# One transformer layer with 32 experts on one core: LayerNorm rows in pieces between the products, the last columns in 256, 128 and 128, part of LayerNorm 2 as a product with a diagonal

## The chip, the cores and the metric

The kernel runs on one core of a Trainium2 chip, as one launch. The metric is the device time of an execution in microseconds (us); lower is better. The profile shows TensorE (PE, with its weight loads as PEld), VectorE (DVE), ScalarE (ACT), GpSimd (POOL) and SyncE (SP), which here issues nearly all transfers from HBM.

## What is computed

One layer over 256 latent tokens of width 1024, in float32, cut to what matters here:

```
o    = bidirectional retention(q, k, v)            # 8 heads, over chunks of 128 tokens
ret  = silu(g) * head_norm(o)                      # norm over the 256 values of a head
z    = silu(layernorm(depthwise_conv(glu)))        # 31 taps
mix  = (ga * (ret @ w_ret_out) + gb * (z @ w_conv_out + b)) @ w_mix_out + b_mix
h    = layernorm(ALPHA * h + gt_m * mix) * ln1_g + ln1_b
u    = modulate(h)
y    = sum over 32 experts of combine[:, e] * ((silu(u @ w_gate[e]) * (u @ w_up[e])) @ w_down[e])
out  = layernorm(ALPHA * h + gt_f * y) * ln2_g + ln2_b
```

A token goes to one group of 8 experts and to two experts in it. All 32 experts' weights (6 MB each, 192 MB in all) are read from HBM.

## The kernel before, in words

Three stages follow one another. The **front** (0 to about 500 us) computes everything up to the router, with float32 products done as three products of high and low parts (`mm3`, lines 94 to 96). The **experts** follow (500 to about 943 us) as 16 pairs `e0 = 0, 2, ... 30`, and then a **tail** (LayerNorm 2 and the store).

*Loads.* `plan` lists the experts' weights as 192 slabs of 1 MB: for each pair eight slabs of `gate` and `up`, then four of `down` (column half `cb` 0 of both experts, then `cb` 1). `slots` names the SBUF buffer of each slab in advance, and `load_to` (line 1016) issues them in that order on SP's queue, which waits for a buffer to be read out before it issues into it. From slab 147 on the buffers form a cycle of 16, earlier one of 18; `NCYC` sets where the shorter cycle begins, since buffers are then wanted for `lnv` (LayerNorm rows) and `yacc` (the sum that becomes the output).

*Front.* `run_steps` goes through a list of steps: each slice of weights is split into high and low parts (`emit`, lines 162 and 163: an ACT copy and a DVE subtraction, `qg`, `qro`, `qco`), `LEAD` slices ahead of PE. `weave` and `call` put the steps of retention, conv norm and gates between one another at positions `APOS`, `TPOS`, ... For the last pair of heads (`p = 3`) `post` (line 667) computes the reciprocal root of the variance by a bit trick and three Newton steps on DVE (lines 113 to 119), while the same for the conv norm (`crs`, 128 x 256) is done by twelve POOL operations (`newton`, lines 820 to 824); `post2` normalises `sr`, which `ret_t` transposes (`rt`, `rT`) as the operand of the product `ya`. `conv_norm` multiplies `zp` by `crs`, `conv_act` makes `zs`, `zh`, `zl`, operands of the product `yb` with the slices `qco` of `wco`. `rows_load` (line 922) broadcasts three rows over the partitions: `b_mix_out`, and two rows of `arow`, a small HBM scratch that POOL writes once the adaLN columns `secs` are there.

*A pair of experts* (`expert_pair`): `hidden` multiplies the gathered 64 tokens of each expert by `gate` and `up` (`gu`, line 1375); `turn` transposes (`ht`); `place` makes the one-hot matrix `sT` that puts the 64 + 64 rows back to their tokens, and the weights `ws` (`st`, lines 1450 and 1452); two down products `dn` (line 1485) are scaled to high and low parts `dh`, `dl` (lines 1497, 1498), which `scatter` of the next pair adds up (`y`, line 1416). Every second pair also gathers the tokens of the next four experts (`ga`, line 1355). PSUM has two banks `mi` for everything small (`ht`, `st`, `dn`, rows), two `gu`, four `y`.

*LayerNorm rows.* The gain and bias rows lie in one partition of `lnv`; a product with a row of ones (`oner`) spreads a row over the 128 partitions. At the end of pair 24 (`LNS[2]`) four such products `l1r` of 512 columns and eight DVE operations make `yacc` out of `xn` and LayerNorm 1's rows. After pair 28 comes the `If` on `cnt_i` (line 1628; not taken here), then four products `l2r` (line 1657) spread LayerNorm 2's rows, and pair 30 begins.

*The last pair* has no scatter into other pairs: after `flush` it runs its down products in pieces of 512, 256 and 256 columns (`p0`, then `dn_1_0`, `dn_1_1`), each weighed (`ds`), put back (`y`), added into `yacc` and sent through `bn_stats` in quarters. Lines 1664 to 1679 finish: `rstd_pair` with a square root on ACT and one Newton step, then half the rows on DVE, half on ACT, POOL and DVE, each quarter stored from SP.

`keep_clock` adds products that nobody reads in the router's waits (`KC0` to `KC4`).

## Time and profile before

| | |
|---|---|
| median of 3 runs | 975.26 us (974.23 to 975.6) |
| the profiled execution | 975.05 us, of which 973.0 us from the first to the last instruction |
| mean granted TensorE clock | 0.984 |
| PE busy | 928.3 us, 95% |
| DVE, ACT, POOL busy | 518.5, 313.2, 100.6 us |
| moved from and to HBM | 294.92 MB, 303 GB/s on the mean, about 420 GB/s while the experts run |

So 2 us lie outside the span. PE is busy nearly all the time and the transfers are at their rate for nearly half of it, so the shares alone do not say which of the two sets the end: that is read stage by stage.

### The profile page before, as it was taken

How to read it: one execution, taken by the hardware profiler on the slowest of the kernel's cores; microseconds unless marked ns; L12 is line 12 of the kernel's file. 1: busy time of each engine (PE TensorE's matmuls, PEld its weight loads, DVE VectorE, ACT ScalarE, POOL GpSimd, SP SyncE). 2: the span in 40 equal slices, each digit the busy share in tenths (PEclk: the TensorE clock that was granted, in tenths of full speed). 3: DMA queues.
4: the chain of work that ended last, by engine and by line, in shares of the span. 5: the costliest groups of instructions: out<-in, count | busy, mean ns of one | idle time of the engine just before them, and what ended most of it. 6: DMA issues, size and time to landing. Idle time of an engine off the chain costs nothing. (4 is left out here: it accounts for less than half of the span.)

```text
span 973.0 us, 15303 instructions
## 1 busy us (share of the span) xinstructions
PE 928.3 (95%) x6327; PEld 688.2 (71%) x6327; DVE 518.5 (53%) x1000; ACT 313.2 (32%) x459; POOL 100.6 (10%) x114
## 2 busy tenths in 40 slices
...
GB/s 352 419 234 252 83 93 194 256 141 184 114 205 224 44 303 228 206 155 313 369 366 314 423 421 421 420 420 421 420 420 422 420 420 420 420 421 420 419 302 44
DMA packets 48744, 294.92 MB, mean 303 GB/s; under 512 B 10304, under 2 KB 10352, under 8 KB 14368
## 3 DMA queue, kind: packets, MB, share of 16 engines
...
q14 instruction: 21, 0.17, 0.0%
HBM read 292.77 MB, written 1.12 MB: 302 GB/s over the span
## 5 line engine op out<-in xcount | busy, mean ns | idle before, releaser
L1375 PE MATMUL gu<-wgate,xe 128*64 128x256 f32 x1024 | 123.0, 391 | 0.7 <-DMA wgate<-in_w_exp_gate_dram 0.5
L1375 PE MATMUL gu<-wup,xe 128*64 128x256 f32 x1024 | 117.7, 380 | 3.4 <-DMA wup<-in_w_exp_up_dram 3.4
L1485 PE MATMUL dn<-wdown,hT 128*64 128x512 f32 (+1 forms) x528 | 117.1, 583 | 3.6 <-DVE hT L1443 2.5
L335 DVE SCALAR_TENSOR_TENSOR slab<-zp,taps,slab 128x256 f32<-128x256 f32 x232 | 109.2, 525 | 0.0
L1375 PEld LDWEIGHTS gu<-wgate,xe 128*64 128x64 f32 x1024 | 74.6, 140 | 45.3 <-issue 9.9
L1381 DVE TENSOR_TENSOR h<-h,gu 128x256 f32<-128x256 f32 x32 | 13.5, 421 | 171.9 <-ACT h L1380 171.9
L1375 PEld LDWEIGHTS gu<-wup,xe 128*64 128x64 f32 x1024 | 73.9, 137 | 41.6 <-DMA wup<-in_w_exp_up_dram 6.6
L1485 PEld LDWEIGHTS dn<-wdown,hT 128*64 128x64 f32 x528 | 40.3, 137 | 68.2 <-issue 58.6
L1380 ACT ACTIVATE h<-gu 128x256 f32<-128x256 f32 x32 | 12.3, 384 | 205.5 <-PE gu L1375 205.5
L1498 DVE SCALAR_TENSOR_TENSOR dl<-dn,ws,ohq 128x512 fp32r<-128x512 f32 x30 | 22.5, 751 | 94.0 <-ACT ohq L1497 94.0
L1497 ACT ACTIVATE ohq<-dn,ws 128x512 fp32r<-128x512 f32 x30 | 20.6, 687 | 130.1 <-PE dn L1485 127.4
L1355 PEld LDWEIGHTS ga<-ohq,xh 128*128 128x128 f32 x224 | 27.9, 188 | 15.9 <-issue 11.1
L95 PE MATMUL ya<-rT,qro 128*128 128x256 f32 x128 | 36.7, 287 | 2.5 <-DVE rT L726 2.5
L75 POOL DMA_DIRECT2D lnv<-in_ln_g_dram x2 | 1.0, 521 | 367.3 <-PE dn L1485 302.8
L96 PE MATMUL glu<-ulh,qz 128*128 128x256 f32 x128 | 36.4, 284 | 1.9 <-DVE qz L163 1.9
L96 PE MATMUL gt<-ulh,qg 128*128 128x256 f32 x128 | 36.2, 283 | 1.9 <-DVE qg L163 1.9
L94 PE MATMUL glu<-ulh,qz 128*128 128x256 f32 x128 | 37.2, 291 | 0.2 <-ACT qz L162 0.2
L96 PE MATMUL ya<-rT,qro 128*128 128x256 f32 x128 | 36.6, 286 | 0.8 <-DVE qro L163 0.8
L1362 DVE TENSOR_SCALAR xe<-ga,cf 128x256 f32<-128x256 f32 x32 | 17.4, 544 | 37.2 <-ACT xe L1365 36.3
L94 PE MATMUL ya<-rT,qro 128*128 128x256 f32 x128 | 37.0, 289 | 0.0
L1355 PE MATMUL ga<-ohq,xh 128*128 128x256 f32 x224 | 33.6, 293 | 3.4 <-DVE dl L1498 3.4
L94 PE MATMUL gt<-ulh,qg 128*128 128x256 f32 x128 | 36.7, 287 | 0.0
...
## 6 DMA issues: line engine op xcount, KB each, us to landing
wgate<-in_w_exp_gate_dram SPq DMA_DIRECT2D x64, 1024.0 KB, 19.8
wup<-in_w_exp_up_dram SPq DMA_DIRECT2D x64, 1024.0 KB, 19.8
wdown<-in_w_down_dram SPq DMA_DIRECT2D x62, 1024.0 KB, 19.8
wa<-in_w_ada_r_dram SPq DMA_DIRECT2D x16, 1024.0 KB, 4.9
wa<-in_w_ada_m_dram SPq DMA_DIRECT2D x8, 1024.0 KB, 14.5
wro<-in_w_ret_out_dram SPq DMA_DIRECT2D x8, 1024.0 KB, 6.9
wg<-in_w_gates_dram SPq DMA_DIRECT2D x8, 1024.0 KB, 7.2
wz<-in_w_glu_dram SPq DMA_DIRECT2D x5, 1024.0 KB, 13.1
```

Source lines behind the costliest of these rows:

```text
L94: T.matmul(ps, st[0], mv[0], start=start, stop=False)
L95: T.matmul(ps, st[0], mv[1], start=False, stop=False)
L96: T.matmul(ps, st[1], mv[0], start=False, stop=stop)
L335: V.scalar_tensor_tensor(dst, zp[:, ct, j:j + NT], taps[:, ct, j:j + 1], ac[ct], op0=ALU.mult, op1=ALU.add)
L1355: T.matmul(ps[:, kk], halves[k // 4][:, s, t, P * (k % 4):P * (k % 4) + P], ohr[:, t], start=(t == 0 and s == 0), stop=(t == 1 and s == 1))
L1362: V.tensor_scalar(xe[c][:, k], ps[:, kk], fsc[:, k:k + 1], fsh[:, k:k + 1], op0=ALU.mult, op1=ALU.add)
L1375: T.matmul(ps[64 * hf:64 * hf + 64, j], xe[c][:, k, CAP * i:CAP * i + CAP], w[:, k % 4, NT * hf:NT * hf + NT], start=start, stop=stop)
L1380: S.activation(h, ps[:, 0], AF.Silu)
L1381: V.tensor_mul(h, h, ps[:, 1])
L1485: T.matmul(ps[64 * x:64 * x + 64], hT[x][:, ch % 2, 64 * (ch // 2):64 * (ch // 2) + 64], w, start=(ch == 0), stop=(ch == 3))
L1497: S.activation(dh, ps, AF.Copy, scale=ws)
L1498: V.scalar_tensor_tensor(dl, ps, ws, dh.bitcast(F32), op0=ALU.mult, op1=ALU.subtract)
```

## The change

The places it touches, and the diff cut to its core.

- *Conv and head norm of `p = 3`*: the reciprocal roots come from ACT's square root, a DVE reciprocal and one Newton step (`rstd_pair`, `conv_root`, `conv_rstd`); the twelve POOL operations are gone; `post2` follows at once, with two of its four operations on ACT; the transposes `rt` come one position earlier.
- *`rows_load`*: the two `arow` broadcasts go to POOL's queue.
- *Mix and router*: the last half of `mx` is kept in two banks of 256 columns, each added as it is done; the constants of `keep_clock` fall; the group's one-hot `og` and a copy of the identity (`iw`) go to POOL.
- *`place`*: identity and router weights lie side by side in `iw`, two products of 192 columns in place of two of 128 and two of 4.
- *LayerNorm rows*: `lnv` and `yacc` are taken at pair 18 in place of pairs 20 and 24, and the 16-slab cycle begins at slab 129. The rows come in 8 + 8 pieces of 256 columns (ACT copy and DVE subtraction of one partition, two products, two DVE operations for LayerNorm 1 or one ACT copy for LayerNorm 2), one at each call of `row()`: four per pair, in pairs 20 and 22, then 24 and 26. The blocks `l1r` and `l2r` are gone.
- *The last pair*: the last 512 columns in pieces of 256, 128, 128 (`ENDS`), with a weight layout of their own, and six of the eight `bn_stats` ahead of the last piece.
- *LayerNorm 2*: two products put the bias into the banks `fo` ahead of time; a diagonal matrix of the reciprocal roots then multiplies the centred rows of the second token half on PE, and ACT copies the sum out. POOL has no part in it.

```diff
-NPOS, APOS, TPOS, QPOS, AHEAD = 7, 9, 7, 5, ()
+NPOS, APOS, TPOS = 7, 9, 6
-NCYC = 130
+NCYC = 112
-LNS = 20, 26, 24, 28
-KC0, KC1, KC2, KC3, KC4 = 0, 2, 3, 4, 4
+LNS = 18, 20, 22, 24
+KC0, KC1, KC2, KC3, KC4 = 0, 0, 2, 2, 3
+ENDS = (0, 256), (256, 128), (384, 128)
...
@@ retain(p): post
-                more = conv_rstd()
...
+            if p < 3:
+                rstd(rs, mv[:, :, 1], 4, f"hn{p}", fill)
+            else:
+                rstd_pair(rs, mv[:, :, 1], "hn3", 4, conv_root)
+            V.scalar_tensor_tensor(nb, mv[:, :, 0], -1.0, rs, op0=ALU.mult, op1=ALU.mult)
+            box["n"] = mv, rs, nb
+            if p == 3:
+                post2()
+                conv_rstd()
...
-            for i in range(4):
+            for i in (1, 0, 3, 2):
                 hh, t = divmod(i, 2)
                 o = sr[:, 1, t, hh * NT:(hh + 1) * NT]
-                V.tensor_scalar(o, box[hh][:, t], mv[:, i, 0:1], rs[:, i:i + 1], op0=ALU.subtract, op1=ALU.mult)
+                if t:
+                    S.activation(o, box[hh][:, t], AF.Identity, scale=rs[:, i:i + 1], bias=nb[:, i:i + 1])
+                else:
+                    V.tensor_scalar(o, box[hh][:, t], mv[:, i, 0:1], rs[:, i:i + 1], op0=ALU.subtract, op1=ALU.mult)
...
+    def conv_root():
+        nbox["rs"], nbox["h"], ve = row1("crs"), row1("crsh"), row1("crsv")
+        V.tensor_scalar(ve, nbox["var"], 1.0 / D, EPS, op0=ALU.mult, op1=ALU.add)
+        S.activation(nbox["rs"], ve, AF.Sqrt)
+        V.tensor_scalar(nbox["h"], ve, -0.5, None, op0=ALU.mult)
+
     def conv_rstd():
...
-            for _ in range(3):
-                G.tensor_mul(t, crs, crs)
-                G.tensor_mul(t, t, ve)
-                G.tensor_scalar(t, t, -0.5, 1.5, op0=ALU.mult, op1=ALU.add)
-                G.tensor_mul(crs, crs, t)
...
+        V.reciprocal(crs, crs)
+        V.tensor_mul(t, crs, crs)
+        V.tensor_mul(t, t, nbox["h"])
+        V.scalar_tensor_tensor(crs, t, 1.5, crs, op0=ALU.add, op1=ALU.mult)
...
     def rows_load(_):
         bcast(tmp[:, 0], a["b_mix_out"][0], D)
-        bcast(tmp[:, 1], arow[0], D)
-        bcast(gtf, arow[1], D)
+        bcast(tmp[:, 1], arow[0], D, nc.gpsimd)
+        bcast(gtf, arow[1], D, nc.gpsimd)
...
@@ expert_pair: place
             for t in range(2):
-                T.matmul(pt[:, t * P:(t + 1) * P], oh[t], identr, start=True, stop=True)
-            for t in range(2):
-                T.matmul(pt[:, NT:NT + 4], oh[t], Wr[:, t, e0 // 2], start=(t == 0), stop=(t == 1))
+                T.matmul(pw[:, t], oh[t], iw[:, t], start=True, stop=True)
...
             hs.append(hidden(e0))
+            row()
             next(side, None)
             hs.append(hidden(e0 + 1))
+            row()
...
                 V.scalar_tensor_tensor(dl, ps, ws, dh.bitcast(F32), op0=ALU.mult, op1=ALU.subtract)
                 places[e0][1][cb] = dh, dl
+                row()
...
@@ expert_pair, last pair
-        down_half(0)
+        down_piece(*ENDS[0])
         for t in range(2):
             py = bank("y", f"y{e0}_0_{t}")
             T.matmul(py, sT[:, t * P:(t + 1) * P].bitcast(F32), ds_[0], start=True, stop=True)
             V.tensor_add(yacc[:, t, 0:512], yacc[:, t, 0:512], py)
-        product(ps[1], 1, half[1])
-        for q in range(2):
+        down_piece(*ENDS[1])
+        add_piece(*ENDS[0])
+        for q in range(3):
             for t in range(2):
                 stats(t, q)
-        down_scale(1)
...
+        down_piece(*ENDS[2])
+        add_piece(*ENDS[1])
+        add_piece(*ENDS[2])
+        for t in (1, 0):
+            stats(t, 3)
...
+    def pieces(n):
+        box = {}
+        def split(i, c):
+            row = lnv[0:1, i, 256 * c:256 * c + 256]
+            h = box["h"] = sb.tile([P, 2, 256], F32R, tag="rope", name=f"lnh{n}{i}{c}", bufs=1)
+            S.activation(h[0:1, 0], row, AF.Copy)
+            V.tensor_sub(h[0:1, 1], row, h[0:1, 0].bitcast(F32))
+        def use(i, c):
+            cs = slice(256 * c, 256 * c + 256)
+            ps = bank("mi", f"ln{n}{i}{c}")[:, 0:256]
+            for j in range(2):
+                T.matmul(ps, oner[0:1], box["h"][0:1, j], start=(j == 0), stop=(j == 1))
+            if n:
+                S.activation(lnv[:, i, cs], ps, AF.Copy)
+                return
...
+    def row():
+        if rows:
+            rows.pop(0)()
...
-        if e0 == LNS[2]:
...
-                    T.matmul(ps, onef[0:1], lnv[0:1, i, cs], start=True, stop=True)
...
-                            V.scalar_tensor_tensor(yk[:, t], pk, ALPHA, xn[:, t, cb], op0=ALU.mult, op1=ALU.mult)
...
+        for n in range(2):
+            if e0 == LNS[2 * n]:
+                rows.extend(pieces(n))
+                rows.pop(0)()
...
@@ LayerNorm 2
-    V.scalar_tensor_tensor(nb2, mv2[:, :, 0], -1.0, rs2, op0=ALU.mult, op1=ALU.mult)
...
-    for E, t, cb in ((V, 0, 0), (V, 0, 1), (G, 1, 1), (V, 1, 0)):
...
+    for cb in range(2):
+        T.matmul(fo[cb], ident, lnv[:, 1, halves[cb]], start=True, stop=False)
...
+    rstd_pair(rs2, mv2[:, :, 1], "l2", 2, lambda: center(1, 0))
+    diag = row1("diag", (P, P))
+    V.tensor_scalar(diag, ident, rs2[:, 1:2], None, op0=ALU.mult)
+    center(1, 1)
+    for cb in range(2):
+        o = yacc[:, 1, halves[cb]]
+        T.matmul(fo[cb], diag, o, start=False, stop=True)
+        S.activation(o, fo[cb], AF.Copy)
+    for cb in range(2):
+        center(0, cb)
+        o = yacc[:, 0, halves[cb]]
+        V.scalar_tensor_tensor(o, o, rs2[:, 0:1], lnv[:, 1, halves[cb]], op0=ALU.mult, op1=ALU.add)
+    for t, cb in ((1, 0), (0, 0), (1, 1), (0, 1)):
+        send(t, cb)
```

The product order on PE (the rows of pair 20 on the changed side are typical of pairs 20 to 26). Before, at the end of pair 24 and the start of pair 26:

```order
L1485 MATMUL dn_1_7123<-wdown_1_6992,hT_7099 64x512
L1645 MATMUL l1r_7150<-lnv,oner 128x512
L1645 MATMUL l1r_7154<-lnv,oner 128x512
L1645 MATMUL l1r_7158<-lnv,oner 128x512
L1645 MATMUL l1r_7162<-lnv,oner 128x512
L1375 MATMUL gu_7182<-wgate_0_6994,xe_6817 64x256 x8
L1375 MATMUL gu_7182<-wgate_1_6996,xe_6817 64x256 x8
L1375 MATMUL gu_7182<-wup_0_6998,xe_6817 64x256 x8
L1375 MATMUL gu_7182<-wup_1_7000,xe_6817 64x256 x8
```

Now, from pair 20's first products on (`ln` are the two products of a piece of a row, `lnh` its high and low parts):

```order
L1383 MATMUL gu_6658<-wup_0_6439,xe_6458 64x256 x8
L1383 MATMUL gu_6658<-wup_1_6441,xe_6458 64x256 x8
L1644 MATMUL ln_6694<-lnh_6645,oner 128x256 x2
L1383 MATMUL gu_6702<-wgate_0_6443,xe_6458 64x256 x8
L1383 MATMUL gu_6702<-wgate_1_6445,xe_6458 64x256 x8
L1383 MATMUL gu_6702<-wup_0_6447,xe_6458 64x256 x8
L1383 MATMUL gu_6702<-wup_1_6449,xe_6458 64x256 x8
L1644 MATMUL ln_6738<-lnh_6699,oner 128x256 x2
L1424 MATMUL y_0_5177<-ohq,sT_6573 128x512
L1424 MATMUL y_0_5177<-dl_0_6590,sT_6573 128x512
```

The four `l1r` that stood in one block are gone, and a piece `ln` stands behind each `gu` group and, further down, behind each `dn` of these pairs.

SP's order around the rows of `arow`. Before:

```order
L78 DMA tmp<-in_b_mix_out_dram 128x1024
L78 DMA tmp<-arow 128x1024
L78 DMA gtf<-arow 128x1024
L72 DMA wco_4326<-in_w_conv_out_dram 128x2048
L72 DMA wco_4387<-in_w_conv_out_dram 128x2048
L72 DMA wgate_0_4452<-in_w_exp_gate_dram 128x2048
```

Now, on SP:

```order
L79 DMA tmp<-in_b_mix_out_dram 128x1024
L73 DMA wco_4324<-in_w_conv_out_dram 128x2048
L73 DMA wco_4385<-in_w_conv_out_dram 128x2048
L73 DMA wgate_0_4450<-in_w_exp_gate_dram 128x2048
L73 DMA wm_0_4452<-in_w_mix_out_dram 128x2048
```

and on POOL:

```order
L900 TENSOR_TENSOR sg_3499<-sg_3499,yaT 128x1024
L76 DMA arow<-secs 128x2x4 x2
L79 DMA tmp<-arow 128x1024
L79 DMA gtf<-arow 128x1024
L900 TENSOR_TENSOR sg_4165<-sg_4165,yaT 128x1024
L930 TENSOR_TENSOR tmp<-tmp 128x1024
```

The two broadcasts moved from SP, where they stood ahead of the conv output weights `wco`, to POOL, behind its own write of `arow`.

DVE's order around the norm of retention's last heads (`qg`, `qro` are the low parts of weight slices that PE waits for). Before:

```order
L117 SCALAR_TENSOR_TENSOR hn3t<-rs_3645 128x4
L118 TENSOR_TENSOR hn3t<-hn3t,hn3v 128x4
L119 SCALAR_TENSOR_TENSOR rs_3645<-hn3t,rs_3645 128x4
L163 TENSOR_TENSOR qg_2_3686<-wg_1_3684,qg_2_3686 128x1024
L697 TENSOR_SCALAR sr_3336<-o_3623,mv_3644,rs_3645 128x256 x2
L697 TENSOR_SCALAR sr_3336<-o_3632,mv_3644,rs_3645 128x256 x2
L700 TENSOR_TENSOR sr_3336<-sr_3336 128x2x256 x2
L163 TENSOR_TENSOR qg_3_3722<-wg_1_3684,qg_3_3722 128x1024
L163 TENSOR_TENSOR qro_0_3753<-wro_0_3751,qro_0_3753 128x1024
```

Now:

```order
L146 SCALAR_TENSOR_TENSOR rs_3650<-hn_2_3662,rs_3650 128x4
L687 SCALAR_TENSOR_TENSOR nb_3651<-mv_3649,rs_3650 128x4
L701 TENSOR_SCALAR sr_3338<-o_3625,mv_3649,rs_3650 128x256
L701 TENSOR_SCALAR sr_3338<-o_3634,mv_3649,rs_3650 128x256
L704 TENSOR_TENSOR sr_3338<-sr_3338 128x2x256 x2
L825 RECIPROCAL crs<-crs 128x256
L826 TENSOR_TENSOR crst<-crs 128x256
L827 TENSOR_TENSOR crst<-crst,crsh 128x256
L828 SCALAR_TENSOR_TENSOR crs<-crst,crs 128x256
L166 TENSOR_TENSOR qg_2_3690<-wg_1_3688,qg_2_3690 128x1024
L166 TENSOR_TENSOR qg_3_3720<-wg_1_3688,qg_3_3720 128x1024
L728 TENSOR_TENSOR rT_3749<-rt_0_3750,rT_3749 128x512
```

The slice `qg_2` moved from ahead of the normalisation `sr` to behind it and behind the four operations on `crs`; `qg_3` follows it at once.

## Rows read from the trace of the kernel before

**Rows 1.** The busy time of each engine in stretches of the span (start:end in us, length; busy us and instructions of PE, PEld, DVE, ACT, POOL; the granted TensorE clock; the mean busy share of the DMA engines; GB/s).

```profile
400.00:405.00 5.00, 2.46 (x12) 2.08 (x11) 4.30 (x3) 4.40 (x7) 1.48 (x1) 0.76 0.87 303
405.00:410.00 5.00, 5.00 (x40) 5.00 (x40) 2.87 (x5) 3.15 (x6) 0.00 (x0) 0.90 0.35 147
430.00:435.00 5.00, 5.00 (x45) 5.00 (x44) 1.95 (x2) 4.13 (x5) 0.00 (x0) 1.00 0.00 0
450.00:455.00 5.00, 1.79 (x8) 1.59 (x9) 2.45 (x2) 3.65 (x5) 1.80 (x4) 0.88 1.01 425
455.00:460.00 5.00, 5.00 (x36) 5.00 (x35) 2.90 (x4) 1.49 (x3) 1.65 (x4) 0.78 1.02 406
525.00:530.00 5.00, 5.00 (x26) 2.89 (x24) 0.75 (x1) 0.69 (x1) 0.00 (x0) 1.00 0.31 128
944.00:945.00 1.00, 1.00 (x14) 0.64 (x12) 0.29 (x1) 0.00 (x0) 0.00 (x0) 1.00 0.08 33
945.00:950.00 5.00, 4.06 (x29) 2.28 (x27) 0.85 (x3) 1.87 (x3) 0.00 (x0) 1.00 0.00 0
```

**Rows 2.** The page's list of DMA issues: instructions of this kind, KB each, median us from issue to landing.

```profile
wgate<-in_w_exp_gate_dram SPq DMA_DIRECT2D x64, 1024.0 KB, 19.8
```

**Rows 3.** PE's timeline, the first product of three consecutive pairs (e0 = 16, 18, 20): start, us, instruction, records merged into the row.

```profile
718.72 3.69 PE L1375 MATMUL gu<-wgate,xe 128*64 128x256 f32 x32
...
742.71 3.62 PE L1375 MATMUL gu<-wgate,xe 128*64 128x256 f32 x32
...
771.82 3.68 PE L1375 MATMUL gu<-wgate,xe 128*64 128x256 f32 x32
```

**Rows 4.** PE's timeline from the second half of the gate product of expert 25 to the start of pair 26 (in brackets the idle time before a row and what ended it).

```profile
840.23 1.95 PE L1375 MATMUL gu<-wgate,xe 128*64 128x256 f32 x16 [0.54 <-DMA wgate<-in_w_exp_gate_dram]
...
845.20 1.95 PE L1375 MATMUL gu<-wup,xe 128*64 128x256 f32 x16 [0.54 <-DMA wup<-in_w_exp_up_dram]
...
858.73 1.12 PE L1645 MATMUL l1r<-lnv,oner 1*128 1x512 f32 x2
...
865.42 6.04 PE L1375 MATMUL gu<-wgate,xe 128*64 128x256 f32 x32
```

**Rows 5.** PE's timeline from the end of pair 28 to the last product.

```profile
922.90 5.40 PE L1657 MATMUL l2r<-lnv,oner 1*128 1x512 f32 x8 [1.81 <-DVEq L1628]
928.24 5.36 PE L1375 MATMUL gu<-wgate,xe 128*64 128x256 f32 x32
...
948.45 5.96 PE L1485 MATMUL dn<-wdown,hT 128*64 128x512 f32 x32
954.34 1.98 PE L1526 MATMUL y<-ds,sT 128*128 128x512 f32 x4
956.25 1.95 PE L1485 MATMUL dn<-wdown,hT 128*64 128x256 f32 x16
```

**Rows 6.** The page's list of costliest groups, the low part `dl` of a down product (busy us, mean ns of one | idle before, and what ended it).

```profile
L1498 DVE SCALAR_TENSOR_TENSOR dl<-dn,ws,ohq 128x512 fp32r<-128x512 f32 x30 | 22.5, 751 | 94.0 <-ACT ohq L1497 94.0
```

**Rows 7.** DVE's timeline in the tail.

```profile
952.72 0.75 DVE L1489 SCALAR_TENSOR_TENSOR ds<-dn,ws,gtf 128x512 f32<-128x512 f32 x1 [3.73 <-PE dn L1485]
...
956.96 1.40 DVE L1509 BATCH_NORM_STATS2 st<-yacc 128x6 f32<-128x256 f32 x4
...
961.61 0.38 DVE L1664 BATCH_NORM_AGGREGATE mv<-st 128x2 f32<-128x24 f32 x2
...
962.47 0.17 DVE L140 RECIPROCAL rs<-rs 128x2 f32<-128x2 f32 x1
...
963.33 0.75 DVE L1677 SCALAR_TENSOR_TENSOR yacc<-yacc,mv,lnv 128x512 f32<-128x512 f32 x1
...
968.84 0.69 DVE L1675 TENSOR_TENSOR yacc<-yacc,lnv 128x512 f32<-128x512 f32 x1
```

**Rows 8.** SP's timeline around the rows of `arow` (instructions that issue transfers).

```profile
421.65 0.60 SPq L78 DMA_DIRECT2D tmp<-in_b_mix_out_dram  x1
441.19 0.33 SPq L78 DMA_DIRECT2D tmp<-arow  x1
...
442.37 0.86 SPq L72 DMA_DIRECT2D wco<-in_w_conv_out_dram  x2
```

**Rows 9.** PE's waits from 380 to 460 us (total us, times, longest).

```profile
PE yb L94 <- ACT qco L162: 2.6, 1, 2.6
PE ya L95 <- DVE rT L726: 2.5, 1, 2.5
PE gt L96 <- DVE qg L163: 1.9, 2, 1.6
```

**Rows 10.** DVE's timeline around the norm of retention's last pair of heads.

```profile
386.60 0.60 DVE L118 TENSOR_TENSOR hn3t<-hn3t,hn3v 128x4 f32<-128x4 f32 x1
...
391.03 1.89 DVE L697 TENSOR_SCALAR sr<-o,mv,rs 128x256 f32<-128x256 f32 x4
...
399.35 3.21 DVE L163 TENSOR_TENSOR qro<-wro,qro 128x1024 fp32r<-128x1024 f32 x1
```

**Rows 11.** POOL's timeline there.

```profile
398.75 2.73 POOL L829 TENSOR_TENSOR zp<-zp,crs 128x1024 f32<-128x1024 f32 x1
```

**Rows 12.** ACT's timeline there.

```profile
401.21 1.28 ACT L838 ACT_TABLE_LOAD   x1
402.50 0.60 ACT L838 ACTIVATE zs<-zp,pcol 128x256 f32<-128x256 f32 x1
```

More of the change, by code (lines that the diff above doesn't have):

```diff
@@ L707, in retain_all @@
         step(lambda _: post2())
-    last = []
     def ret_t(p, c2):
@@ L1478, in expert_pair, with product @@
         ds_ = {}
-        def product(ps, cb, cs):
+        def product(ps, cb, c):
             for ch in range(4):
                 for x in range(2):
-                    w = wts[e0 + x, "down", cb][:, ch]
-                    w = w[:, cs.start // 256] if cs.stop - cs.start == 256 else w
+                    w = wts[e0 + x, "down", cb]
+                    w = w[c][:, ch] if last and cb else w[:, ch]
                     T.matmul(ps[64 * x:64 * x + 64], hT[x][:, ch % 2, 64 * (ch // 2):64 * (ch // 2) + 64],
@@ L1499, in expert_pair @@
                 places[e0][1][cb] = dh, dl
+                row()
             next(side, None)
             return
-        half = [slice(256 * q, 256 * q + 256) for q in range(2)]
-        ps = [bank("gu", f"dn{e0}_1_{q}")[:, 0:256] for q in range(2)]
         ds_[1] = sb.tile([P, 512], F32, tag="b2", name=f"ds{e0}_1", bufs=2)
@@ L1617, in tile_block, with one_, go @@
     lnv = yacc = None
+    def pieces(n):
[13 more added lines that the diff above has]
+                return
+            r, o = divmod(c, 2)
+            for t in range(2):
+                if i == 0:
+                    V.scalar_tensor_tensor(yacc[:, t, cs].rearrange("p (q k) -> p k q", k=4),
+                                           ps.rearrange("p (q k) -> p k q", k=4), ALPHA,
+                                           xn[:, t, r, :, 64 * o:64 * o + 64], op0=ALU.mult, op1=ALU.mult)
+                else:
+                    V.scalar_tensor_tensor(yacc[:, t, cs], ps, ALPHA, yacc[:, t, cs], op0=ALU.mult, op1=ALU.add)
+        todo = [(i, c) for i in range(2) for c in range(4)]
+        def one_(j):
+            def go():
+                if j:
+                    use(*todo[j - 1])
+                if j < len(todo):
+                    split(*todo[j])
+            return go
+        return [one_(j) for j in range(len(todo) + 1)]
+    def row():
+        if rows:
+            rows.pop(0)()
+    rows = []
     for e0 in range(0, NE, 2):
```

196 lines of the change are left out of this document (85 added, 111 removed).

## The prediction

> **What bounds the kernel now.** I read the stretches of the span first, then PE's waits and timeline from the end backwards, then the front.
>
> In the experts' stage two clocks run against each other. One is the transfers: a slab of 1 MB becomes usable every 2.49 us (840.23 and 845.20 are two slabs apart, each product behind an idle of 0.54 us for its slab [rows 4]), so a pair of 12 slabs takes 29.9 us. Counted on from there, slab n is usable at 840.23 + 2.49 (n - 149): the first of pair 20 (n = 120) at 768.0, of pair 30 (180) at 917.4, the last up slab (187) at 934.9, the last `cb0` slab (189) at 939.8, the very last (191) at 944.8. The bytes confirm it: 8% of the rate from 944 to 945, nothing after [rows 1]. The other clock is PE: a pair without gathers takes 742.71 - 718.72 = 24.0 us, one with them 771.82 - 742.71 = 29.1 [rows 3]. PE starts pair 20 3.8 us behind the transfers, and by 840 it waits for each slab.
>
> It loses that step at the end of pair 24. The four `l1r` and their DVE operations run from 858.73 to 865.42, and the next gate product takes 6.04 us where it took 3.62 [rows 3, 4]. Slab 156 was usable at 857.7, so pair 26 starts 7.7 us late. Before pair 30 PE idles 1.81 us, spends 5.40 on `l2r` and 5.36 on a gate product [rows 5]: that product begins at 928.24, 10.8 after its slab. The last down product begins at 948.45, with its second expert's operand some 0.5 later, so I count from 949.0; its slabs were there at 939.8. Hence **at the end PE, not the transfers, is late, by 9.2 us**.
>
> The transfers' own schedule was fixed much earlier. From 430 to 435 nothing is moved, from 525 to 530 31% [rows 1]: buffers come free as PE reads them. From about 535 the rate is full to the end, so whatever PE gains before then moves every later slab with it.
>
> **The change, part by part.**
>
> *LayerNorm rows.* Removed: the two blocks. Added: 16 pieces over pairs 20 to 26. A piece's two products cover half of an `l1r`'s columns (a row of two records is 1.12 us for 512 [rows 4], at a low clock): 0.3 to 0.6 us. Larger is what they wait for. With two `mi` banks a piece between `dn_0` and `dn_1` makes `dn_1` take the bank of `dn_0`, so PE waits until `dl` has read it: 0.75 us [rows 6] behind the piece's own products, about 1 us a pair. In pair 20 `yacc`'s first write waits for the buffer's last reader, about 1.5; in pair 22 the gathers queue behind a bank that DVE must clear, about 2. I take +2.8, +4, +2, +2.2 us for the four pairs, 11 in all. Transfers set 917.4 - 771.8 = 145.6 us from PE's start of pair 20 to slab 180; PE needs 3 x 24.0 + 2 x 29.1 = 130.2 there. The slack of 15.4 holds 11, and pair 28, which has no piece, ends in waiting. So pair 30 follows the transfers: slab 187 at 934.9, 16 records of 1.9 us, 2.0 for `h` and its transposes, 938.8; slab 189 at 939.8. **The last down product starts at 939.8, not 949.0: -9.2** (bounds: -7, if 2 us of wait stay in pair 30; -9.2, since slab 189 excludes more).
>
> *Fewer buffers.* Sixteen slabs ahead are 39.8 us of transfers; one takes 19.8 from issue to landing [rows 2]. The schedule starves only if PE falls some 19 us behind; the worst I find is 4. Cost 0, hidden under that margin.
>
> *Place.* Two products of 192 columns for two of 128 and two of 4: about -0.25 us a pair, nothing where PE waits for slabs.
>
> *`arow` on POOL's queue.* SP issues `b_mix_out` at 421.65 and then stands until 441.19, since `arow` is not there; the two `wco` slices go out at 442.37 [rows 8]. They arrive late: PE idles 2.6 us for `qco` [rows 9], and the clock of the next ten microseconds is 0.88 and 0.78 [rows 1], which is 0.6 + 1.1 = 1.7 us of full speed. With SP free, `wco` lands in the idle stretch around 430. POOL has only the `sg` product queued behind, which waits for ACT later. Gain 4.3; bounds 0 (another wait, on DVE's low parts, takes the place) and 4.5.
>
> *Norm of the last heads.* DVE's operations are stretched beside POOL's Newton steps: a 128 x 4 multiply takes 0.60, then `qro` 3.21 beside POOL's 2.73 [rows 10, 11]. PE waits 1.9 for `qg` and 2.5 for `rT` [rows 9] and then runs at 0.76 and 0.90 [rows 1], 1.7 more: 6.1 at most. Now POOL's twelve are gone, but `qg_2` stands behind the normalisation and four `crs` operations. Adding up DVE's queue from the variance (385.7): small operations 1.9, ACT's root 0.4, `sr` 0.8 (half of 1.89 [rows 10]) and 1.4, `crs` 1.6, `qg_2` 1.2 gives 393.0, where it ended at 391.1: a new stall of about 2 us takes the place of the old 1.9. What goes is the `rT` stall. ACT has one more table load, 1.28 us [rows 12], ahead of `zs`, which pushes the conv operands by about 1. I take -2.5, bounds -0.5 and -5.
>
> The Trainium skill speaks against a part of this: "VectorE: DVE Perf Modes" (First, the fixed hardware budget) says that Reciprocal iterates with a repeat count of 8. By it the one over 256 columns would be an estimated 256 x 8 / 0.96 GHz = 2.1 us; no row here is wide enough to show it (0.17 us for two columns [rows 7], as short as any operation). In my sum it stands at 0.3, the time of a plain operation of that width; by the page `qg_2` ends 1.8 later and the term falls to about -0.7. The same holds for ACT: "ScalarE: Activation LUTs" (What ACT_TABLE_LOAD costs) adds a drain of 1.38 us to each switch, but `zs` begins at 402.50, 0.01 after the load's end [rows 12], so the row decides.
>
> *Mix and router.* Earlier sums for the norm, fewer fillers, `og` on POOL: -0.2 (bounds -0.7 and +0.3, a clock that sinks with the fillers gone); `st` in pair 0 -0.3.
>
> Together **the front moves every slab by 2.5 + 4.3 + 0.5 = 7.3 us** (3 to 10).
>
> *Tail.* From the start of the last down product to the end of the last DVE operation it is 968.84 + 0.69 - 949.0 = 20.5 us. In the new order the pieces of 128 columns need 16 records each; at 256 columns they take 1.95 / 16 = 0.12 [rows 5]. I take 0.11, since the weight load does not shrink (bounds 0.06, by columns, and 0.12). Counted from the start: 512 and 256 columns to 5.3, `y` to 7.2 (its 1.98 [rows 5]), the first piece of 128 to 9.0, its `y` to 10.0, two adds to 10.9, six statistics of 0.35 [rows 7], which now stand ahead of the last `ds`, to 13.0, that `ds` 0.4, four small adds 1.1, two statistics 0.7: `bn_aggr` starts at 15.2, in place of 961.61 - 949.0 = 12.6. The end is shorter: centre 0.75 under ACT's root, five small operations 1.0, the diagonal 0.3, then five operations of 0.75 [rows 7], with `aggr`'s 0.4 and the first two steps' 0.2 some 6.4 in place of 7.9. Sum 15.2 + 6.4 = 21.6, **+1.1**, which I round to +1.2 for the stores, whose order changes (bounds 0 and +2.5, when the diagonal's products on PE, at low clock, come last).
>
> **Sum.** 975.05 - 9.2 - 7.3 + 1.2 = **959.8 us**. The profiled execution lies 0.2 under the median of the runs, 975.26.
>
> **Rivals.**
> 1. *The front gives nothing*: `qg_2` behind a slow reciprocal stalls PE as long as `rT` did, and `yb` waits for ACT's later `zs` whatever `wco` does. For it: DVE and ACT are full there. Against: a stall of 2.6 has a transfer alone behind it. 975.05 - 9.2 + 1.2 = 967.1. Chance 0.15.
> 2. *The pieces keep PE behind*: at 1.4 us each they cost 22, 6.6 over the slack, and pair 30 starts late as now. For it: two `mi` banks. Against: only four a pair, with ACT and DVE idle. 975.05 - 9.2 + 6.6 - 7.3 + 1.2 = 966.4. Chance 0.1.
> 3. *The tail gets shorter*: pieces of 128 by columns, full clock: -1.5 in place of +1.2, 957. Chance 0.1.
> 4. *Slower: each piece costs over 1.9 us*, in pairs 20 to 26, since ACT's and DVE's split, PE and the copy out of the bank run one after another with PE standing behind them. The point is where 16 pieces eat the slack, the old lateness and the front's gain less the tail: (15.4 + 9.2 + 7.3 - 1.2) / 16 = 1.9. At 2.2, 35.2 - 15.4 = 19.8 late: 975.05 + 10.6 - 7.3 + 1.2 = 979.6, and close to the 19 us at which buffers run out too. For it: an `l1r` with its DVE work cost 6.7 / 4 = 1.7 [rows 4]. Against: the split is done a position ahead, and only two of four calls in a pair stand before a product that needs the same bank. Chance 0.04.
> 5. *Nothing moves the end*: front and rows each give back what they take, 975. Chance 0.03.
>
> The forecast itself has 0.58, with a range of its own of 955 to 964. Faster by over 0.2% (2 us, about what a measurement of this kernel tells from no change) is the forecast and rivals 1 to 3: 0.92; within it 0.04; slower 0.04. For 8 in 10 the range runs from 954 to 969, the bounds of the front and rivals 1 and 2 inside.
>
> **What would show it.** In the changed trace: no PE wait for `qco` near 450, `wco` issued before 430, transfers flowing from 427 on; full rate about 7 us earlier than 535; pair 30's gate products each behind a wait for their slab; the last byte near 937 and the last down product within 3 us of slab 189; 21 to 22 us from its start to the last DVE operation. I am wrong if PE has no slab wait in pair 28, if the idle before `ya` or `yb` is over 3 us, or if the last byte lands later than 942.

## The result and the profile after

The changed kernel takes 962.57 us (median of four runs, 961.19 to 963.65) where the kernel before takes 975.10 beside it: a ratio of 0.9872, with a 95% interval of 0.9855 to 0.9889. In a second measurement, further down, the ratio was 0.9863 (0.9840 to 0.9886). The forecast was 959.8, with a range of 954 to 969. The profiled execution takes 962.40 us with a span of 960.6, 12.4 less than before.

Three places carry the argument. First the front, in the same view as [rows 1]: busy us and instructions of PE, PEld, DVE, ACT and POOL, the granted clock, DMA share, GB/s.

```profile
395.00:400.00 5.00, 4.36 (x24) 4.36 (x25) 5.00 (x4) 0.11 (x1) 2.62 (x1) 0.66 0.15 23
400.00:405.00 5.00, 5.00 (x45) 5.00 (x44) 3.64 (x5) 3.67 (x6) 0.00 (x0) 1.00 0.87 329
...
430.00:435.00 5.00, 5.00 (x44) 5.00 (x44) 1.84 (x4) 4.13 (x5) 0.00 (x0) 1.00 0.32 134
490.00:495.00 5.00, 4.14 (x19) 3.05 (x18) 3.52 (x15) 4.47 (x4) 1.00 (x4) 0.61 1.00 405
495.00:500.00 5.00, 5.00 (x18) 3.83 (x19) 0.54 (x1) 0.97 (x2) 0.00 (x0) 0.71 1.01 424
```

The low clock of 400 to 410 and of 450 to 460 is gone. Two new stretches of it have come: 395 to 400, and the router from 490 to 500, where it was 1.00 before. PE's waits from 380 to 460 (to be laid beside [rows 9]) show one stall in place of three, and a wait for `zl` of 1.1 us where it was 0.2:

```profile
PE gt L97 <- DVE qg L166: 3.2, 1, 3.2
PE yb L96 <- DVE zl L842: 1.1, 1, 1.1
```

SP's timeline around `wco`: no row of `arow`, and the first `wco` slice goes out 15 us earlier than in [rows 8].

```profile
422.18 0.38 SPq L79 DMA_DIRECT2D tmp<-in_b_mix_out_dram  x1
427.27 7.60 SPq L73 DMA_DIRECT2D wco<-in_w_conv_out_dram  x2
434.96 0.39 SPq L73 DMA_DIRECT2D wgate<-in_w_exp_gate_dram  x1
```

Then PE at the end, in the view of [rows 5]:

```profile
917.02 3.67 PE L1383 MATMUL gu<-wgate,xe 128*64 128x256 f32 x32 [1.80 <-DVEq L1684]
...
935.41 1.07 PE L1495 MATMUL dn<-wdown,hT 128*64 128x512 f32 x2
936.78 5.34 PE L1495 MATMUL dn<-wdown,hT 128*64 128x512 f32 x30 [0.30 <-DMA wdown<-in_w_down_dram]
...
946.05 1.09 PE L1495 MATMUL dn<-wdown,hT 128*64 128x128 f32 x16
```

The last down product now waits for its slab (189, which lands at 936.6), with PE idle for 0.3 us: at that place the transfers are the later of the two. And DVE's tail, in the view of [rows 7]:

```profile
940.44 0.75 DVE L1499 SCALAR_TENSOR_TENSOR ds<-dn,ws,gtf 128x512 f32<-128x512 f32 x1 [4.49 <-PE dn L1495]
...
951.00 0.38 DVE L1719 BATCH_NORM_AGGREGATE mv<-st 128x2 f32<-128x24 f32 x2
...
956.10 0.75 DVE L1731 SCALAR_TENSOR_TENSOR yacc<-yacc,rs,lnv 128x512 f32<-128x512 f32 x1
```

**Where the time went.** I followed the start of the same products in both traces (us, before and after):

| PE reaches | before | after | shift |
|---|---|---|---|
| `o` of the last pair of heads | 377.49 | 378.62 | +1.13 |
| the gate products behind the first `yb` | 426.94 | 427.47 | +0.53 |
| `mx` | 466.46 | 461.55 | -4.91 |
| the router's first gather `ga` | 499.73 | 494.65 | -5.08 |
| the first gate product of pair 0 | 503.35 | 499.90 | -3.45 |
| the first `ds` (DVE) of the last pair | 952.72 | 940.44 | -12.28 |
| end of the span | 973.0 | 960.6 | -12.40 |

So the front gave 3.45 us, the rows 12.28 - 3.45 = 8.83, and the tail 0.12. The forecast had 7.3, 9.2 and -1.2. The two executions begin alike (PE's short stall near 50 stands at 49.15 and 49.24), so these shifts hold to 0.1 us.

Two parts of the change show neither a gain nor a loss. From the first gate product of pair 0 to that of pair 20 it is 268.47 us in both kernels, so the shorter `place` did not speed up these ten pairs. And slab 189 lands at 936.6 in place of 940.1, earlier by as much as the front gave: the transfers lost nothing by the fewer buffers.

### The profile page after: what moved, and what is told of

It reads as the page before. It is cut to its first block, busy times and chain, and to the rows that moved or that the text cites. A ratio compares the mean times of both kernels' runs of the same rounds, so it can differ in the third digit from the quotient of the medians.

```text
span 960.6 us, 15381 instructions
## 1 busy us (share of the span) xinstructions
PE 919.7 (96%) x6339; PEld 684.2 (71%) x6339; DVE 525.4 (55%) x1022; ACT 324.5 (34%) x492; POOL 92.5 (10%) x104
## 3 DMA queue, kind: packets, MB, share of 16 engines
q0 software_dynamic: 1072, 1.74, 0.7%
## 4 chain that ended last, share of the span: by engine, by line
PE 77%; DMA 13%; DVE 6%; ACT 3%; issue 1%; POOL 0%; DVEq 0%; ACTq 0%; SPq 0%; POOLq 0%
PE gu L1383 18%; PE dn L1495 9%; DMA wdown<-in_w_down_dram 4%; DMA wgate<-in_w_exp_gate_dram 4%; DMA wup<-in_w_exp_up_dram 4%; PE o L663 3%; PE y L1424 2%; PE ga L1363 2%; PE glu L97 2%; PE glu L95 2%; PE adp L773 2%; PE glu L96 1%; PE gt L97 1%; PE sc L644 1%; PE gt L95 1%; PE gt L96 1%
## 5 line engine op out<-in xcount | busy, mean ns | idle before, releaser
L1495 PE MATMUL dn<-wdown,hT 128*64 128x512 f32 (+2 forms) x544 | 116.9, 571 | 8.6 <-DVE hT L1451 4.4
L1383 PE MATMUL gu<-wgate,xe 128*64 128x256 f32 x1024 | 117.7, 381 | 1.8 <-DVEq L1684 1.8
L336 DVE SCALAR_TENSOR_TENSOR slab<-zp,taps,slab 128x256 f32<-128x256 f32 x232 | 114.7, 547 | 0.0
L1383 PEld LDWEIGHTS gu<-wgate,xe 128*64 128x64 f32 x1024 | 72.4, 137 | 40.7 <-issue 2.8
L97 PE MATMUL ya<-rT,qro 128*128 128x256 f32 x128 | 36.1, 282 | 0.8 <-DVE qro L166 0.8
L96 PE MATMUL gt<-ull,qg 128*128 128x256 f32 x128 | 36.6, 286 | 0.0
L95 PE MATMUL ya<-rT,qro 128*128 128x256 f32 x128 | 36.2, 283 | 0.0
L96 PE MATMUL glu<-ull,qz 128*128 128x256 f32 x128 | 36.1, 282 | 0.0
```

The costliest lines, as they stand in the source:

```text
L95: T.matmul(ps, st[0], mv[0], start=start, stop=False)
L96: T.matmul(ps, st[0], mv[1], start=False, stop=False)
L97: T.matmul(ps, st[1], mv[0], start=False, stop=stop)
L336: V.scalar_tensor_tensor(dst, zp[:, ct, j:j + NT], taps[:, ct, j:j + 1], ac[ct], op0=ALU.mult, op1=ALU.add)
L1383: T.matmul(ps[64 * hf:64 * hf + 64, j], xe[c][:, k, CAP * i:CAP * i + CAP], w[:, k % 4, NT * hf:NT * hf + NT], start=start, stop=stop)
L1495: T.matmul(ps[64 * x:64 * x + 64], hT[x][:, ch % 2, 64 * (ch // 2):64 * (ch // 2) + 64], w, start=(ch == 0), stop=(ch == 3))
```

## The experiments

An execution's start scatters: the same early product stood between 48.7 and 50.9 us in the traces of all these kernels. So I compare times by their ratio to the kernel before on the same chip, and places in a trace by distances inside it.

**The `arow` broadcasts alone**, in the kernel before:

```diff
-    def bcast(dst, src, n):
+    def bcast(dst, src, n, queue=nc.sync):
...
-        bcast(tmp[:, 1], arow[0], D)
-        bcast(gtf, arow[1], D)
+        bcast(tmp[:, 1], arow[0], D, nc.gpsimd)
+        bcast(gtf, arow[1], D, nc.gpsimd)
```

> The kernel before, with the two `arow` broadcasts on POOL's queue and nothing else. Theory (the 2.63 us wait for `qco` and the clock that falls with it are all of SP's standing still, and in the kernel before PE is late at the end, so that the gain arrives whole): no wait for `qco`, clock 1.00 from 450 to 460, `mx` starts at 461.5 in place of 466.5, the end 5 us earlier: about 970 us. The forecast's term was 4.3: 970.8. Rival (the transfers of the experts' first slabs are no earlier, so pair 0 waits for them): less than 1.5 us, 973.6 or more.

Measured: 969.31 us beside 973.78, ratio 0.9945 (0.9927 to 0.9962). From the gate products behind the first `yb` to the second `yb` PE takes 22.72 us in place of 25.51, from there to `mx` 11.36 in place of 14.01: 2.79 + 2.65 = 5.44, the same 5.44 as in the changed kernel (+0.53 to -4.91). The waits for `qco` are gone:

```profile
PE ya L95 <- DVE rT L726: 2.5, 1, 2.5
PE gt L96 <- DVE qg L163: 1.9, 2, 1.6
PE yb L95 <- DVE zl L840: 0.2, 1, 0.2
```

The theory stands, and the term was under-sized: behind the 2.6 us for `qco` there was a second wait of 0.8 for its low part, and the low clock cost about 2.0. This trace is also 1.25 us shorter from `ya` to the first `yb` (14.49 in place of 15.74), which the edit does not touch: the waits there are the same, but the granted clock from 400 to 410 is 1.00, where the kernel before had 0.76 and 0.90 [rows 1].

**`qg_2` ahead of the `crs` operations**, in the changed kernel:

```diff
                 post2()
+                next_slice()
                 conv_rstd()
```

> The changed kernel with the weight slice `qg_2` converted right behind `sr`, ahead of the four operations on `crs`. Theory (the reciprocal over 256 columns, 1.74 us, and its followers stand between PE and `qg_2`, but behind that wait the conv operands zs, zh, zl set the start of `yb`): PE's wait of 3.16 us at 395.6 falls to about 0.4, `crs` comes 1.2 us later, and `yb` starts no earlier than 414.0 (414.46 now), or waits more inside: at most 1 us reaches pair 0, the time is 961.5 to 962.8. Rival (the wait alone costs the time): all of 2.8 us arrive, the first gate product of pair 0 at 497.1, the time at 959.8.

Measured: 957.57 us, ratio 0.9830 (0.9794 to 0.9866); the interval overlaps the changed kernel's (0.9855 to 0.9889) a little, but on this chip its runs (956.53 to 958.75) lie below all those of the kernels of the next two experiments (960.36 to 964.23), which differ from the changed kernel in fillers or in one tile. My theory fell. The rival held in kind, the wait does cost the time, but was too small: it had 2.8 us, and from the stall near 50 to the first gate product it is 444.85 us in place of 450.66, 5.8 less. In the changed kernel DVE did this between the variance and the slices PE waits for:

```profile
390.12 1.28 DVE L704 TENSOR_TENSOR sr<-sr 128x512 f32<-128x512 f32 x2
391.33 1.74 DVE L825 RECIPROCAL crs<-crs 128x256 f32<-128x256 f32 x1
393.11 0.42 DVE L826 TENSOR_TENSOR crst<-crs 128x256 f32<-128x256 f32 x1
...
394.36 4.34 DVE L166 TENSOR_TENSOR qg<-wg,qg 128x1024 fp32r<-128x1024 f32 x2
```

With the slice ahead, its row stands at 391.59 and the reciprocal behind it:

```profile
391.59 1.22 DVE L166 TENSOR_TENSOR qg<-wg,qg 128x1024 fp32r<-128x1024 f32 x1
392.73 1.75 DVE L826 RECIPROCAL crs<-crs 128x256 f32<-128x256 f32 x1
```

PE's wait falls from 3.2 to 0.6, and the clock from 395 to 400 is 1.00 in place of 0.66:

```profile
PE yb L96 <- DVE zl L843: 1.0, 1, 1.0
PE gt L97 <- DVE qg L166: 0.6, 1, 0.6
```

From the first `rt` to `ya` PE takes 7.84 us in place of 11.46, and only 0.34 of these 3.62 are given back from `ya` to `yb`. Most of the rest of the 5.8 us comes from the router: there the first gather takes 3.62 us to the first gate product in this kernel, with the few fillers, where the changed kernel takes 5.25.

**The fillers as before**, in the changed kernel:

```diff
-KC0, KC1, KC2, KC3, KC4 = 0, 0, 2, 2, 3
+KC0, KC1, KC2, KC3, KC4 = 0, 2, 3, 4, 4
```

> The changed kernel with the constants of keep_clock as before (0, 2, 3, 4, 4 in place of 0, 0, 2, 2, 3). Theory (the missing fillers let the clock fall in the router): the first gather `ga` takes 3.7 us again in place of 5.3, the granted clock from 490 to 500 is 1.00 in place of 0.61 and 0.71, the first gate product of pair 0 comes 1.5 us earlier (498.4), the end too: about 961.0 us. Rival (the fillers delay the router's own products by as much as the clock gives back): the first gate product within 0.4 us of 499.9, the time at 962.5.

Measured: 961.82 us, ratio 0.9868 (0.9831 to 0.9904), not told apart from the changed kernel by time. The trace does show the mechanism at its place. The changed kernel, and then this one:

```profile
494.65 5.32 PE L1366 MATMUL ga<-ohr,xn 128*128 128x256 f32 x16
```

```profile
495.51 3.69 PE L1366 MATMUL ga<-ohr,xn 128*128 128x256 f32 x16
```

From the last `ut` before `plog` (485.15 and 485.97) to the first gate product it is 14.75 and 13.16 us: 1.6 back. In the same execution the way from `rt` to `ya` was 1.3 longer (12.72), with the clock at 0.50 from 395 to 400 and 0.87 behind, although nothing there differs. So the clock behind the 3.2 us stall at `qg` scatters, by about as much as the fillers bring. That their gain reaches the time is not shown here: the other three runs had a higher mean clock (0.998 in place of 0.995) and took 960.36 to 962.50 us.

**`l2` and `l3` in two tiles, and in buffers of their own.** The 1.13 us ahead of `o` were in no step of mine. The trace has a new wait of PE for `qwq` (1.2 us, at 90.5), and it goes back to ACT:

```profile
80.61 0.22 ACT L251 ACTIVATE l<-l 128x16 f32<-128x16 f32 x1
81.89 1.28 ACT L257 ACT_TABLE_LOAD   x1 [1.06 <-DVE l L255]
83.18 0.22 ACT L257 ACTIVATE l<-l 128x16 f32<-128x16 f32 x1
```

A part of the change that is not in the diff shown makes `l2` and `l3` of the decay rates (in ACT's Ln) two halves of a tile `l23` that rotates with others. First I gave each half a tile of its own in the same rotation:

```diff
-        l23 = row1("l23", (P, 2, 16))
-        l2, l3 = l23[:, 0], l23[:, 1]
+        l2, l3 = row1("l2", (P, 16)), row1("l3", (P, 16))
```

> The changed kernel, with `l2` and `l3` of decay_rates in two tiles in place of two halves of one tile `l23`. Theory (the shared tile makes ACT's Ln wait for DVE's last read of the other half): ACT's idle of 1.06 us before its table load at 81.9 goes, the products `o` of the last heads start 1.1 us earlier (377.5 in place of 378.6), the first gate product of pair 0 at 498.8 in place of 499.9, the end 1.1 us earlier: about 961.4 us. Rival (the 1.1 us are a difference between executions, or come from something else that moved): `o` stays at 378.6 and the time at 962.5.

Measured: 962.87 us, ratio 0.9885 (0.9849 to 0.9921), the wait for `qwq` is 1.3 us, and ACT is idle for 1.13 before the same load. The sharing of a tile was not it. ACT's instruction order with its waits (semaphores by name) says what is. Before:

```
L256 ACT_TABLE_LOAD
L256 ACTIVATE l_91<-l_91 128x16 [waits DVE_49]
```

and after:

```
L257 ACT_TABLE_LOAD [waits DVE_49]
L257 ACTIVATE l_901<-l_901 128x16 [waits Activation_49]
```

A rotating buffer brings a second wait (for its earlier user), and the wait for DVE then stands on the table load, which could have run ahead. So the second edit takes the buffers out of the rotation:

```diff
-    l1 = small((16,), "l1")
+    l1, l2, l3 = small((16,), "l1"), small((16,), "l2"), small((16,), "l3")
...
-        l23 = row1("l23", (P, 2, 16))
-        l2, l3 = l23[:, 0], l23[:, 1]
```

> The changed kernel, with `l2` and `l3` in buffers of their own again (as in the kernel before), in place of a buffer that rotates with other tiles. In the instruction order of the changed kernel ACT's Ln has two waits, of which the one on DVE stands on its table load; with own buffers the table load has none. Theory: the table load starts at 80.8 in place of 81.9, PE's wait of 1.2 us for `qwq` near 90 goes, the time is 1.1 us less: about 961.4. Rival (that wait is absorbed before pair 0 by DVE or ACT): the time stays at 962.5 and the products `o` of the last heads at 378.6.

ACT's rows in this kernel:

```profile
81.94 0.22 ACT L249 ACTIVATE l<-l 128x16 f32<-128x16 f32 x1
82.17 1.28 ACT L255 ACT_TABLE_LOAD   x1
```

The load follows at once, no wait for `qwq` is left, and from the last stall before (49.24 and 50.57) to the next one at `v0p` (94.75 and 95.04) it is 44.47 us in place of 45.51; 44.47 is also what the kernel before has. These 1.04 us are shown. That they reach the end is not: 962.04 us, ratio 0.9863 (0.9845 to 0.9880), overlaps the changed kernel's, and the router's gather took 5.57 this time.

**The rows in their two blocks**, in the changed kernel (the blocks, the buffers' pairs and the 16-slab cycle of the kernel before):

```diff
-NCYC = 112
+NCYC = 130
-LNS = 18, 20, 22, 24
+LNS = 20, 26, 24, 28
...
-                rows.extend(pieces(n))
-                rows.pop(0)()
...
+                    T.matmul(ps, onef[0:1], lnv[0:1, i, cs], start=True, stop=True)
...
```

> The changed kernel with LayerNorm's rows in the two blocks of the kernel before (`l1r` behind pair 24, `l2r` ahead of pair 30, buffers and the 16-slab cycle as before). Theory (the blocks make PE late at the end, the slabs come as in the changed kernel): the last down product 9 us later, the time 8.9 us more: about 971.4. Rival (the pieces cost PE as much in sum as the blocks, and the front alone made the kernel faster): less than 3 us more, 965 or less.

Measured: 971.44 us beside 974.15, ratio 0.9967 (0.9952 to 0.9981), against 0.9872: 9.2 us more. From the stall near 50 to the end it is 970.7 - 50.85 = 919.85 us, in the changed kernel 960.6 - 49.24 = 911.36: 8.5. Slab 189 lands where it did (887.2 us behind that stall, 887.4 in the changed kernel), but the last down product begins 9.3 us later (895.45 in place of 886.17) and waits for no slab. The block is back, behind the wait at the `If`:

```profile
920.88 5.42 PE L1713 MATMUL l2r<-lnv,oner 1*128 1x512 f32 x8 [1.81 <-DVEq L1684]
```

The rows' term is shown, at 8.5 to 9.2.

**More work in each piece.**

```diff
+            for _ in range(2):
+                T.matmul(ps[:, 0:P], ident, onef, start=True, stop=True)
             for j in range(2):
                 T.matmul(ps, oner[0:1], box["h"][0:1, j], start=(j == 0), stop=(j == 1))
```

> The changed kernel with two more products of 128 x 128 that nobody reads in each of the 16 pieces of a row, about 0.6 us a piece, 10 us in all. By the forecast's slack (4.4 us left at pair 30 and 3 us inside it) the end moves by 2 to 3 us: 965. By the changed kernel's trace (PE starts pair 30 3.0 us behind its slab and waits 0.3 us in the last down product and 0.9 in pair 26) it moves by 8 to 9: 971.

Measured: 966.86 us, ratio 0.9919 (0.9902 to 0.9935), 4.6 us more; by the distances inside the trace 4.2. Neither number was met, but the trace tells why. From the start of pair 20 to pair 30 PE takes 153.7 us in place of 148.65, so of some 10 us of products (64 records, 0.65 us a piece) only 5 came through. Of the rest, 2.8 us fell into waits that PE had at the pieces anyway, and 1.7 into waits for slabs in pairs 26 and 28, which are gone. These are PE's waits from 760 to 900, in the changed kernel

```profile
PE dn L1495 <- DVE dl L1508: 2.3, 2, 1.2
PE ga L1363 <- DVE dl L1508: 1.7, 2, 1.2
...
PE ln L1644 <- DVE lnh L1638: 1.1, 1, 1.1
PE gu L1383 <- DMA wup<-in_w_exp_up_dram: 0.9, 2, 0.5
```

and with the added products

```profile
PE dn L1495 <- DVE dl L1508: 1.1, 2, 0.5
PE ga L1363 <- DVE dl L1508: 1.1, 2, 0.5
...
PE ln L1646 <- DVE lnh L1638: 0.5, 1, 0.5
```

The two down products of pair 28, which the changed kernel runs in 7.94 us, take 7.09 as in the kernel before:

```profile
914.43 7.09 PE L1495 MATMUL dn<-wdown,hT 128*64 128x512 f32 x32 [0.32 <-DVE hT L1451]
```

Counted from the stall near 50, pair 30 begins 4.9 us later and the first `ds` 4.2, since the wait for slab 189 is gone too. So the changed kernel had room for 0.9 us each in pairs 26 and 28 and for 0.7 in the last pair, not the 7 of the forecast's slack.

**The tail.** First the whole tail of the kernel before, put back into the changed one:

```diff
-ENDS = (0, 256), (256, 128), (384, 128)
+ENDS = (0, 256), (256, 256)
...
-    fo = [bank("mi", f"fo{cb}") for cb in range(2)]
...
+    for E, t, cb in ((V, 0, 0), (V, 0, 1), (G, 1, 1), (V, 1, 0)):
...
```

> The changed kernel with the tail of the kernel before: last columns in 256 and 256, LayerNorm 2 on DVE, ACT and POOL. By the forecast the old tail is 1.2 us shorter: 961.4. By the changed trace (16.4 us from the first `ds` to the last DVE operation, 16.8 before) it is 0.4 longer: 963.0. A third theory, that the pieces of 128 start the last product earlier since their slabs land in smaller parts, would add up to 1.2 more: 964.

Measured: 962.14 us, ratio 0.9870 (0.9847 to 0.9892), span 960.4: no difference from the changed kernel, and the time alone does not tell the three theories apart. The third falls by the trace: from the stall near 50 to the first `ds` it is 891.27 us, in the changed kernel 891.20. Its first `ds` starts at 940.45 and its last DVE operation ends 16.8 us later, 0.4 behind the changed kernel's 16.4; the stores then take 0.6 less. Then the old pieces with the new LayerNorm 2:

```diff
-ENDS = (0, 256), (256, 128), (384, 128)
+ENDS = (0, 256), (256, 256)
...
-        down_piece(*ENDS[2])
...
-            stats(t, 3)
+        weigh(ds_[1][:, 256:512], ps1, slice(768, 1024))
...
```

> The changed kernel with the last columns in 256 and 256 as before (adds and statistics in the old order), but with the new LayerNorm 2. Theory (the two halves of the tail cancel: the pieces of 128 make bn_aggr start 1.7 us later, 10.56 in place of 8.89 after the first `ds`, the new LayerNorm 2 is 2.1 us shorter, 5.85 in place of 7.92 from bn_aggr to the last DVE operation): from the first `ds` to the last DVE operation 14.7 us in place of 16.4, the time 1.7 us less than the changed kernel. Rival (the stores of the new order, or the products with the diagonal, come last whatever the pieces do): within 0.5 us of the changed kernel.

Measured: 961.77 us, ratio 0.9852 (0.9828 to 0.9876), beside 0.9863 for the changed kernel on that chip. From the first `ds` to the last DVE operation it is 14.9 us, 1.5 less, as the theory says, but the span ends 4.2 after it in place of 3.75, since the products with the diagonal ran at a low clock (0.87 and 0.79 from 950 to 960, in the changed kernel 1.00 and 0.87) and ACT's copies and the stores came last:

```profile
953.17 3.32 PE L1732 MATMUL fo<-yacc,diag 128*128 128x512 f32 x4 [2.24 <-DVE diag L1728]
```

(1.98 us in the changed kernel). So about 1 us arrives, which the times alone do not tell from nothing.

**All of it together**: own buffers, the slice ahead, the old pieces with the new LayerNorm 2.

```diff
+ENDS = (0, 256), (256, 256)
...
+    l1, l2, l3 = small((16,), "l1"), small((16,), "l2"), small((16,), "l3")
...
+                next_slice()
...
```

> The changed kernel with three edits together: own buffers for l2 and l3, `qg_2` converted ahead of the `crs` operations, last columns in 256 and 256. Theory: 1.0 + 3.6 to 5.8 (the larger, if the clock stays up in the router) + 1.7 us less than the changed kernel: 6.3 to 8.5, about 954 to 956 us. Rival (the transfers, not the front, set the last slab, so that only the tail's part arrives): 1.7 us less, 961.

The same with the fillers:

```diff
-KC0, KC1, KC2, KC3, KC4 = 0, 0, 2, 2, 3
+KC0, KC1, KC2, KC3, KC4 = 0, 2, 3, 4, 4
```

> The same three edits with the constants of keep_clock as in the kernel before. If the clock falls in the router without the fillers (first gather 5.3 us in place of 3.6), this is 1 to 1.6 us faster than the kernel with the three edits alone; if it stays up there (as it did with `qg_2` moved), the fillers cost 0.3 us.

And the changed kernel beside them, without an edit:

> The changed kernel itself, beside the three kernels above on one chip: 0.9872 of the kernel before as measured first (interval 0.9855 to 0.9889).

Measured on one chip, beside 975.45 for the kernel before: the changed kernel 962.43 (0.9863, 0.9840 to 0.9886), the three edits 956.19 (0.9797, 0.9769 to 0.9824), with the fillers 954.91 (0.9788, 0.9765 to 0.9811). The three edits gave 6.2 us, just under the 6.3 to 8.5 expected; the rival (961) fell. The fillers' part is not told from nothing by the times, but the traces show it. In the router, without the fillers and with them:

```profile
489.39 5.62 PE L1365 MATMUL ga<-ohr,xn 128*128 128x256 f32 x16
```

```profile
489.61 3.69 PE L1365 MATMUL ga<-ohr,xn 128*128 128x256 f32 x16
```

The two programs are alike up to the router's last `ut` (480.05 and 480.08), and their first gate products stand at 494.95 and 493.24: the fillers are worth 1.7 us when the clock falls. The last kernel is faster than both given ones, by 0.8% and 2.1%.

## Why the prediction was right, and where it was not

The forecast came 2.8 us too low, 12.4 where the sum had 15.3. Its main step held; three of its terms did not. Their errors have two signs: the front fell short by 3.9 us and the rows by 0.4, the tail gave 1.3 more than forecast. That the total came so near is in part luck.

1. *PE is late at the end, and the spread rows cure it*: right. The step had -9.2; the trace gives -8.83, and the blocks put back cost 8.5 to 9.2. In the changed kernel the last down product waits for slab 189, as forecast, and the step's calculation of that slab holds: by the two slab waits at 869.32 and 871.81 (slabs 162 and 163) it is due at 871.81 + 26 x 2.49 = 936.6, and the product goes on at 936.78.
2. *The cost of the pieces*: the path was right, the size too small, and the result did not show it. The pairs took 28.7, 32.6, 26.8, 33.6 and 25.0 us where 24.0 and 29.1 alternate: 16.5 more. Of these, 0.9 are waits for slabs in pair 26 and 0.9 in pair 28, at its last down product. There the list of PE's waits shows nothing, since the other expert's products run on in the meantime; the weight loads show it:

```profile
907.28 7.94 PE L1495 MATMUL dn<-wdown,hT 128*64 128x512 f32 x32 [0.31 <-DVE hT L1451]
911.57 0.20 PEld L1495 LDWEIGHTS dn<-wdown,hT 128*64 128x64 f32 x4 [0.67 <-DMA wdown<-in_w_down_dram]
```

   So the pieces cost some 15 us where the forecast had 11 (0.9 each, rival 2 had 1.4), the slack of 15.4 just held them, and pair 28 did end in waiting: my sign of an error, "no slab wait in pair 28", is not there. What I left out are the waits behind `dn` in front of the next gather (1.2 us, for `dl`) and for the next split row (1.1). I also left out that PE must begin pair 30 behind its slab whatever the pieces cost. When the last slab of pair 28 has landed (911.5), PE still has 3.65 us of down products and the 1.8 us of the `If` ahead of it, and the next slab lands after 2.5. So it begins at 917.02, 2.9 us behind, and makes this up inside the pair: it needs 18.4 us to the last down product, the nine slabs up to 189 need 22.4.
3. *The front*: -3.45 in place of -7.3. This is the step that failed. The queue gave 5.4 for 4.3. The norm gave 0.6 for 2.5: the sum had the reciprocal at 0.3 us, as a plain operation of that width, and it took 1.74. The stall was 3.2 us in place of 2, and the clock fell behind it, which I had not counted. "VectorE: DVE Perf Modes" of the Trainium skill (First, the fixed hardware budget), by which I had worked out an estimate of 2.1 us and a term of -0.7, was the nearer one: the trace has 1.74 us and -0.6. Even these 0.6 lie within the clock's scatter, since the kernel with the `arow` edit alone has 1.25 less in the same stretch by its clock. The router cost 1.5 in place of a gain of 0.5: I had the fallen clock as a bound of +0.3, and one gather at that clock costs 1.6. And 1.1 us were lost near 90 us, in an edit of buffers that I had set at nothing without looking at the waits it brings.
4. *The tail*: -0.1 in place of +1.2. The shape was right (`bn_aggr` 1.7 us later, the end 2.1 shorter), both sizes were off: from the start of the last down product on slab 189 (936.78) to the last DVE operation it is 20.1 us, where the sum had 21.6. The 16 products of 128 columns take 1.09 us, 0.07 each and not 0.11: they do get cheaper with their columns.

Since the front gave less, the last bytes moved between 941 and 942 (a DMA share of 0.02, nothing after), not near 937, and so only just inside the limit of 942 that I had named. The stall of 3.2 us came ahead of a gate product `gt`, where no sign of mine looked.
